# A decoder layer's last MLP pass: the third chunk of columns taken in two halves, its last half finished by VectorE alone

## The chip, the cores and the metric

The kernel runs on one core of a Trainium2 chip. The metric is the device time of one launch in microseconds (us), from runs outside the profiler; one more execution was recorded by the hardware profiler, and its trace is what the rows below come from. TensorE multiplies matrices and writes to PSUM, VectorE and ScalarE work element by element on SBUF and PSUM, GpSimd works on SBUF alone, and SyncE issues most of the DMAs.

## The reference

One layer of a decoder trunk for 1024 prompt tokens and 8 sample tokens: an attention and a convolution branch, a merge, and a squared-ReLU MLP with a norm on either side. The change lies in the last lines, the second MLP product, its norm and the residual sum:

```python
def _rms_norm(x, g):
    xf = x.astype(jnp.float32)
    y = xf * lax.rsqrt(jnp.mean(xf * xf, axis=-1, keepdims=True) + EPS)
    return (y * g.astype(jnp.float32)).astype(x.dtype)
...
    x = x + _rms_norm(mix, g_mix_post)
    h = _rms_norm(x, g_ffn_pre)
    f = jnp.square(jax.nn.relu(h @ w_ff1)) @ w_ff2
    return x + _rms_norm(f, g_ffn_post)
```

`w_ff1` is 1024 x 4096 and `w_ff2` 4096 x 1024. All data are float32.

## The kernel before, in words

Everything is kept transposed: a tile has 128 features as partitions and tokens as columns. The 1032 tokens (`T`) are three chunks of 344 columns (`CH`), and the 1024 output features are eight blocks of 128 (`m` from 0 to 7). So that products come out in float32 precision, each weight and each activation is split into a high and a low part, and each product of 128 features is three matmuls (`mac`, lines 257, 260 and 261): high by high, high by low, low by high.

The second MLP product sums over 4096 hidden features. It is taken in 15 passes of `ff2`. The first 14 take 256 hidden features each and go block by block, chunk by chunk, each adding into the SBUF tile `f`. The last pass (`chunk_major`) takes the last 512 hidden features and goes chunk by chunk: for a chunk it runs the eight blocks in order, so that a chunk of `f` is complete when its eighth block is. For one block of one chunk (`one`), TensorE runs 12 matmuls of 344 columns into one of four PSUM banks, and VectorE adds the bank to `f` (line 1419). ScalarE then squares the block (line 1387) and scales it by the gain (line 1433). The squares of the blocks are added into two running sums (line 1393; of blocks 2 and 4 on GpSimd in the first two chunks, elsewhere on VectorE; in the third chunk blocks 6 and 7 are not added, but summed by TensorE as they are).

When a chunk is complete, `finish` normalises it and writes it out. TensorE sums the squares over the features, with the 344 columns as three blocks of 128 (`sum_rows`, line 304); a chain of tiny VectorE operations and a square root on ScalarE make the factor per token (`rms_rows`, lines 315 to 325); TensorE spreads the factors over all partitions (`spread`, line 331). Then, in four steps of two feature blocks each, VectorE multiplies by the factor (line 1458), the residual is added (line 1461; on GpSimd or VectorE, by step) and SyncE issues the DMA to the output (line 1462). `finish` is a generator: for the first two chunks it is stepped once after each block of the next chunk, so its work stands between the blocks of the next chunk in every engine's queue. For the third chunk nothing comes after it, and it runs by itself at the end.

`pin` and `pe` keep the written order on each engine. `tick` moves the stream of weights along: it issues loads, and splits loaded weights into high and low parts (lines 177 and 180) ahead of their use. `r2` and `r4` hold factors per token that were made in earlier passes by `mlp_factors`.

Of the kernel before, what the change touches and what calls it, by code (L numbers as in the profile page):

```python
# [10 lines left out]
F32 = mybir.dt.float32  # L11
F32R = mybir.dt.float32r
AF = mybir.ActivationFunctionType
OP = mybir.AluOpType
# [4 lines left out]
P = 128  # L19
KT = 8  # L20
NQ = 1024
NB = 8
T = NQ + NB
CH = T // 3
HT = T // 2
ST = HT // 2
EPS = 1e-6
NEG = -1e30

def chunk(c):  # L30
    return slice(c * CH, (c + 1) * CH)
# [6 lines left out]
def tile_decoder_layer(  # L38
# [5 lines left out]
    nc = tc.nc  # L44
# [7 lines left out]
    small = ctx.enter_context(tc.tile_pool(name="small", bufs=2))  # L52
    mm = ctx.enter_context(tc.tile_pool(name="mm", bufs=1, space=PSUM))
# [50 lines left out]
    for i in range(0, KT, 2):  # L104
        m = 36 + 3 * i
# [21 lines left out]
    sums = {}  # L127
# [28 lines left out]
    for key in plan:  # L156
        keys, fs = forms_of(key)
# [141 lines left out]

    NB3 = ((0, 128), (128, 128), (CH - 128, 128))  # L300

    def sum_rows(ps, sq, first, last):
        for b, (o, w) in enumerate(NB3):
            pe(nc.tensor.matmul(ps[:, b:b + 1], sq[:, o:o + w], ones, start=(first and b == 0),  # L304
                                stop=(last and b == 2), skip_group_check=True))

    def rms_rows(ps, s2=None, s4=None):


        var = small.tile([P, 3], F32, name="var")  # L310
        ri = small.tile([P, 3], F32, name="ri")
        if s2 is None:
            pin(nc.vector.tensor_scalar(var, ps[:, 0:3], 1.0 / NQ, EPS, op0=OP.mult, op1=OP.add))
        else:
            pin(nc.vector.tensor_tensor(var, ps[:, 0:3], s4, op=OP.mult))
            pin(nc.vector.tensor_scalar(var, var, EPS, None, op0=OP.add))
        sd = small.tile([P, 3], F32, name="sd")
        pin(nc.scalar.activation(sd, var, AF.Sqrt))
        pin(nc.vector.reciprocal(ri, sd))
        t = small.tile([P, 3], F32, name="nt")  # L320
# [7 lines left out]
    def spread(ri):  # L328
        rb = bank(at, [P, 512], "ps_rb")
        for b, (o, w) in enumerate(NB3):  # L330
# [1041 lines left out]

    with tc.tile_pool(name="ff", bufs=1, side="right") as ff:
        f = ff.tile([P, KT, T], F32, name="f")
        r2 = [ff.tile([P, 3], F32, name=f"r2_{c}") for c in range(3)]
        r4 = [ff.tile([P, 3], F32, name=f"r4_{c}") for c in range(3)]

        def squares_of(src, last=KT):


            res = [None, None]
            for k in range(KT):
                new = k < 2 or k >= last
                nm = "fac" if new else "fsq"
                pool, bufs = (ff, 2) if len(spaces) < 3 else (spaces[2][0], 8)
                sq = pool.tile([P, CH], F32, name=nm, tag=nm, bufs=bufs)
# [9 lines left out]
        def add_sums(ps, tiles, first=True, last=True):  # L1396
            for i, a in enumerate(tiles):
                sum_rows(ps, a, first and i == 0, last and i == len(tiles) - 1)

        def ff2(prs, chunk_major):  # L1400
            hs = [hidden.pop(pr) for pr in prs]
            ws = {}

            def one(m, c):
                ps = bank(mm, [P, CH], "ps_mm")
                if m % 4 == 0 and c == 0:
                    ws[m // 4] = [take(("wf2", 2 * pr + a, m // 4)) for pr in prs for a in range(2)]
                mac(ps, [((w[0][:, m % 4], w[1][:, m % 4]), (rh[:, a, chunk(c)], rl[:, a, chunk(c)]))
                         for w, (a, (rh, rl)) in zip(ws[m // 4], ((a, h) for h in hs for a in range(2)))])
                if m % 4 == 3 and c == 2:  # L1410
                    for w in ws[m // 4]:
                        retire(w)
                if chunk_major or (3 * m + c) % 2:
                    tick()
                d = f[:, m, chunk(c)]
                if prs[0] == 0:
                    nc.scalar.copy(d, ps)
                else:
                    pin(nc.vector.tensor_tensor(d, ps, d, op=OP.add))  # L1419
            if not chunk_major:  # L1420
                for m in range(KT):
                    for c in range(3):
                        one(m, c)
                return
            done = iter(())
            for c in range(3):
                end = c == 2
                sq = squares_of(lambda k: f[:, k, chunk(c)], 6 if end else KT)
                for m in range(KT):
                    one(m, c)  # L1430
                    sums = next(sq)
                    fm = f[:, m, chunk(c)]
                    pin(nc.scalar.activation(fm, fm, AF.Copy, scale=gn[:, 3, m:m + 1]))  # L1433
                    run(done, 1)
                    if end and m == 6:
                        ps = bank(at, [P, 512], "ps_ss")
                        add_sums(ps, sums[:2], True, False)
                run(done)
                if not end:
                    ps = bank(at, [P, 512], "ps_ss")  # L1440
                done = finish(c, ps, sums)
            run(done)

        def finish(c, ps, sums):
            end = c == 2
            if end:
                add_sums(ps, sums[2:], False)
            else:
                yield
                add_sums(ps, sums)  # L1450
            ri = rms_rows(ps, r2[c], r4[c])
            if not end:
                yield
            rb = spread(ri)[:, None, 0:CH].to_broadcast([P, 2, CH])
            vs_ = [f[:, k:k + 2, chunk(c)] for k in range(0, KT, 2)]

            def scale(j):
                pin(nc.vector.tensor_tensor(vs_[j], vs_[j], rb, op=OP.mult))  # L1458

            def out(j, eng):  # L1460
                pin(eng.tensor_tensor(vs_[j], vs_[j], x2[c][:, 2 * j:2 * j + 2, :], op=OP.add))  # L1461
                pin(nc.sync.dma_start(yT[:, 2 * j:2 * j + 2, chunk(c)], vs_[j]))
            scale(0)
            out(0, nc.gpsimd)
            yield
            scale(1)
            out(1, nc.gpsimd)
            yield
            scale(2)
            out(2, nc.vector if end else nc.gpsimd)  # L1470
            yield
            scale(3)
            out(3, nc.vector)
            yield

        def mlp_factors(c):

            for sums in squares_of(lambda k: x2[c][:, k, :]):
                yield
            pin(nc.gpsimd.tensor_tensor(sums[0], sums[0], sums[1], op=OP.add))  # L1480
            yield
            yield
            ps = bank(at, [P, 512], "ps_ss")
            add_sums(ps, sums[0:1])
            ri = rms_rows(ps)
            pin(nc.vector.tensor_tensor(r2[c], ri, ri, op=OP.mult))
            pin(nc.vector.scalar_tensor_tensor(r4[c], r2[c], 1.0 / NQ, r2[c], op0=OP.mult, op1=OP.mult))
# [94 lines left out]
```

## Time and profile before

| | before |
|---|---|
| median of 3 runs | 2033.48 us (2033.07 to 2035.68) |
| the profiled execution, its own time | 2032.52 us |
| its span, first to last instruction | 2030.7 us, so 1.8 us of its time lie around it |
| busy in the span: TensorE, VectorE, ScalarE, GpSimd | 1955.0, 1243.6, 735.3, 602.6 us |
| mean granted TensorE clock | 0.983 of full |

Busy time is the time in which an engine worked on an instruction; matmuls are pipelined, so that a matmul's duration is longer than the distance to the next one's start. The second number of a row of the timeline is a duration in us; "x2" are two instructions in one row, with the time from the first's start to the last's end.

### The profile page before, as it was taken

Reading aid. Unit: us, or ns where it says so; the run is one execution under the profiler, and the core shown is the slowest. Engines: PE = TensorE matmul, PEld = TensorE weight load, DVE = VectorE, ACT = ScalarE, POOL = GpSimd, SP = SyncE. Lnnn points to the kernel's source line nnn. Section 1 sums busy time; section 2 is a strip of 40 time slices with the busy share of each in tenths; the row PEclk is TensorE's granted clock in tenths of the full one; section 3 lists DMA queues with packets and bytes.
Section 4 is the critical chain, followed back from the end, with each engine's and each line's share of the span. In section 5 each row is a group of like instructions: output and inputs, shape, how many; then the busy total and the mean of one; then the engine's idle time right before and its main releaser. Section 6 shows DMA issues by size and latency. Waiting matters only on the chain. (4 is left out here: it accounts for less than half of the span.)

```text
span 2030.7 us, 33252 instructions
## 1 busy us (share of the span) xinstructions
PE 1955.0 (96%) x13253; PEld 1932.2 (95%) x13253; DVE 1243.6 (61%) x2086; ACT 735.3 (36%) x1448; POOL 602.6 (30%) x487
## 2 busy tenths in 40 slices
PE   7999999999998899999999999999999999999996
PEld 6999999999998799999999999999999999999995
DVE  7688768777756787897554423735544444454545
ACT  4355435544442333333343333452222222222242
POOL 3233313332334674662412222211111111111113
PEclk8999999999999899999999999999999999999998
DMA  4221343144334363331665431322222322222102
GB/s 146 59 87 38 108 131 128 59 129 131 111 101 164 113 205 109 126 116 54 186 251 165 138 102 46 94 91 86 84 94 84 125 94 84 94 94 83 53 22 84
DMA packets 85995, 216.74 MB, mean 107 GB/s; under 512 B 12000, under 2 KB 22368, under 8 KB 84944
## 3 DMA queue, kind: packets, MB, share of 16 engines
q1 hardware_dynamic: 68736, 119.12, 18.2%
q10 hardware_dynamic: 8112, 68.78, 10.0%
q0 software_dynamic: 8992, 26.72, 4.4%
q8 instruction: 104, 1.70, 0.3%
q14 instruction: 51, 0.42, 0.1%
HBM read 184.17 MB, written 84.86 MB: 132 GB/s over the span
## 5 line engine op out<-in xcount | busy, mean ns | idle before, releaser
L180 POOL TENSOR_TENSOR wl<-wr,wh 128x512 fp32r<-128x512 f32 x152 | 201.9, 1329 | 804.4 <-ACT wh L177 707.6
L177 ACT CAST wh<-wr 128x512 fp32r<-128x512 f32 x320 | 195.3, 619 | 526.5 <-PE ps_mm L260 272.4
L257 PE MATMUL ps_mm<-hh,wh 128*128 128x344 f32 x1008 | 329.7, 327 | 2.5 <-ACT hh L346 1.9
L260 PE MATMUL ps_mm<-hl,wh 128*128 128x344 f32 x1008 | 324.2, 322 | 3.7 <-DVE hl L340 1.9
L261 PE MATMUL ps_mm<-hh,wl 128*128 128x344 f32 x1008 | 323.4, 321 | 0.0
L261 PE MATMUL ps_mm<-rh,wl 128*128 128x344 f32 x768 | 246.4, 321 | 0.0
L257 PE MATMUL ps_mm<-rh,wh 128*128 128x344 f32 x768 | 246.4, 321 | 0.0
L260 PE MATMUL ps_mm<-rl,wh 128*128 128x344 f32 x768 | 245.7, 320 | 0.0
L260 PE MATMUL ps_mm<-gl,wh 128*128 128x344 f32 x768 | 244.9, 319 | 0.8 <-DVE gl L1303 0.8
L257 PE MATMUL ps_mm<-gh,wh 128*128 128x344 f32 x768 | 245.5, 320 | 0.0
L261 PE MATMUL ps_mm<-gh,wl 128*128 128x344 f32 x768 | 244.7, 319 | 0.0
L1419 DVE TENSOR_TENSOR f<-ps_mm,f 128x344 f32<-128x344 f32 x336 | 170.4, 515 | 111.5 <-PE ps_mm L261 110.9
L180 DVE TENSOR_TENSOR wl<-wr,wh 128x512 fp32r<-128x512 f32 x168 | 139.7, 832 | 152.8 <-ACT wh L177 152.4
L260 PEld LDWEIGHTS ps_mm<-hl,wh 128*128 128x128 f32 x1008 | 190.8, 189 | 5.7 <-DVE hl L340 3.2
L257 PEld LDWEIGHTS ps_mm<-hh,wh 128*128 128x128 f32 x1008 | 191.2, 190 | 3.9 <-ACT hh L346 2.9
L261 PEld LDWEIGHTS ps_mm<-hh,wl 128*128 128x128 f32 x1008 | 190.7, 189 | 0.0
L260 PEld LDWEIGHTS ps_mm<-gl,wh 128*128 128x128 f32 x768 | 144.2, 188 | 1.2 <-DVE gl L1303 1.1
L260 PEld LDWEIGHTS ps_mm<-rl,wh 128*128 128x128 f32 x768 | 144.8, 189 | 0.0
L261 PEld LDWEIGHTS ps_mm<-rh,wl 128*128 128x128 f32 x768 | 144.8, 189 | 0.0
L257 PEld LDWEIGHTS ps_mm<-rh,wh 128*128 128x128 f32 x768 | 144.8, 189 | 0.0
L257 PEld LDWEIGHTS ps_mm<-gh,wh 128*128 128x128 f32 x768 | 144.3, 188 | 0.0
L261 PEld LDWEIGHTS ps_mm<-gh,wl 128*128 128x128 f32 x768 | 144.1, 188 | 0.0
(326 smaller groups left out, 4555.0 us busy)
## 6 DMA issues: line engine op xcount, KB each, us to landing
wr<-in_win_dram SPq DMA_DIRECT2D x152, 256.0 KB
wr<-in_wf_dram SPq DMA_DIRECT2D x128, 256.0 KB
out_okv_dram<-in_cache_dram ACTq DMA_DIRECT2D x16, 1020.0 KB
kt<-in_cache_dram SPq DMA_DIRECT2D x32, 256.0 KB
x_sb<-in_xT_dram SPq DMA_DIRECT2D x12, 344.0 KB
cv_d<-D SPq DMA_DIRECT2D x16, 258.0 KB
gr<-g_d POOLq DMA_DIRECT2D x8, 516.0 KB, 7.4
cv<-cv_d ACTq DMA_DIRECT2D x8, 516.0 KB
```

What stands on the lines that cost most here:

```text
L177: pin_(nc.scalar.copy(hi, raw))
L180: pin_(eng.tensor_tensor(lo, raw, hi.bitcast(F32), op=OP.subtract))
L257: ins = nc.tensor.matmul(ps, wh, rh, start=(first and i == 0), stop=False)
L260: nc.tensor.matmul(ps, wh, rl, start=False, stop=False)
L261: nc.tensor.matmul(ps, wl, rh, start=False, stop=(last and i == n - 1))
L1419: pin(nc.vector.tensor_tensor(d, ps, d, op=OP.add))
```

## The change

The third chunk becomes two pieces of 172 columns (`HC`), so the last pass has four pieces (`LAST`): two of 344 columns and two of 172. Each half runs its own eight blocks, its own sums (two blocks of columns, the second 44 wide) and its own `finish`; that of the first half is stepped between the blocks of the second half. In both halves all four residual additions are VectorE's; the first two chunks keep theirs. Only the last half keeps the third chunk's treatment of the squares, while the first half adds the squares of blocks 2 and 4 on GpSimd as the first two chunks do. The call of `tick` moves from before VectorE's addition into `f` to after it, in all 15 passes.

```diff
-    def sum_rows(ps, sq, first, last):
-        for b, (o, w) in enumerate(NB3):
+    def sum_rows(ps, sq, first, last, blocks=NB3):
+        for b, (o, w) in enumerate(blocks):
...
+        HC = CH // 2
+        HB = ((0, 128), (HC - 128, 128))
+        LAST = [(0, 0, CH, NB3, slice(0, 3)), (1, 0, CH, NB3, slice(0, 3)),
+                (2, 0, HC, HB, slice(0, 2)), (2, HC, HC, HB, slice(2, 4))]
...
-                if chunk_major or (3 * m + c) % 2:
-                    tick()
-                d = f[:, m, chunk(c)]
+                d = f[:, m, s]
...
-            for c in range(3):
-                end = c == 2
-                sq = squares_of(lambda k: f[:, k, chunk(c)], 6 if end else KT)
+            for j, (c, o, n, blocks, fs) in enumerate(LAST):
+                end = j == len(LAST) - 1
+                s = slice(CH * c + o, CH * c + o + n)
+                sq = squares_of(lambda k: f[:, k, s], 6 if end else KT, n)
                 for m in range(KT):
-                    one(m, c)
+                    one(m, s, j == 0, end)
+                    tick()
                     sums = next(sq)
...
-            scale(0)
-            out(0, nc.gpsimd)
-            yield
...
-            out(2, nc.vector if end else nc.gpsimd)
-            yield
-            scale(3)
-            out(3, nc.vector)
-            yield
+            for j in range(4):
+                scale(j)
+                out(j, nc.vector if n < CH or j == 3 else nc.gpsimd)
+                yield
```

On VectorE, the end of the program before: eight rows from the addition of the last two blocks on (`ps_mm` is a block's bank, `ps_ss` the sums, `ps_rb` the spread factors, `x_2` the residual of the third chunk).

```order
L321 SCALAR_TENSOR_TENSOR nt<-ri 128x3
L323 TENSOR_TENSOR ri<-ri,r_2_14351 128x3
L324 TENSOR_TENSOR nt<-nt,var 128x3
L325 SCALAR_TENSOR_TENSOR ri<-nt,ri 128x3
L1458 TENSOR_TENSOR f<-f,ps_rb 128x2x344 x3
L1461 TENSOR_TENSOR f<-f,x_2_12969 128x2x344
L1458 TENSOR_TENSOR f<-f,ps_rb 128x2x344
L1461 TENSOR_TENSOR f<-f,x_2_12969 128x2x344
```

On VectorE now, two blocks in the middle of the second half, where the first half's `finish` is stepped.

```order
L1424 TENSOR_TENSOR f<-ps_mm,f 128x172
L1399 TENSOR_TENSOR fac<-fac,fsq 128x172
L1467 TENSOR_TENSOR f<-f,ps_rb 128x2x172
L1470 TENSOR_TENSOR f<-f,x_2_12969 128x2x172
L1424 TENSOR_TENSOR f<-ps_mm,f 128x172
L1399 TENSOR_TENSOR fac<-fac,fsq 128x172
L1467 TENSOR_TENSOR f<-f,ps_rb 128x2x172
L1470 TENSOR_TENSOR f<-f,x_2_12969 128x2x172
```

A round of block, square sum, scaling and residual now stands four times on VectorE in the second half, and the program ends with four pairs of scaling and residual of two times 172 columns in place of the eight rows' last six operations.

On GpSimd, the end of the program before.

```order
L1461 TENSOR_TENSOR f<-f,x_0_12967 128x2x344 x2
L1393 TENSOR_TENSOR fac<-fac,fsq 128x344
L1461 TENSOR_TENSOR f<-f,x_0_12967 128x2x344
L1461 TENSOR_TENSOR f<-f,x_1_12968 128x2x344 x3
L1461 TENSOR_TENSOR f<-f,x_2_12969 128x2x344 x2
```

And now.

```order
L1470 TENSOR_TENSOR f<-f,x_0_12967 128x2x344 x2
L1399 TENSOR_TENSOR fac<-fac,fsq 128x344
L1470 TENSOR_TENSOR f<-f,x_0_12967 128x2x344
L1399 TENSOR_TENSOR fac<-fac,fsq 128x172
L1470 TENSOR_TENSOR f<-f,x_1_12968 128x2x344 x2
L1399 TENSOR_TENSOR fac<-fac,fsq 128x172
L1470 TENSOR_TENSOR f<-f,x_1_12968 128x2x344
```

GpSimd's last operation was a residual addition of the third chunk; now it is one of the second chunk, which stands beside the blocks of the first half.

## Rows read from the trace of the kernel before

**Rows 1.** The page's costliest groups: one kind of MLP matmul and its idle time.
```profile
L257 PE MATMUL ps_mm<-rh,wh 128*128 128x344 f32 x768 | 246.4, 321 | 0.0
```

**Rows 2.** The chain of work that ended last, parts of it: start, us, what.
```profile
1996.58 0.16 PE ps_mm L260
...
2009.13 0.29 PE ps_mm L260
...
2012.54 0.02 issue
...
2019.29 1.41 DVE f L1461
```

**Rows 3.** The sequencers' instructions behind the program (L1565): duration in ns min/median/max.
```profile
L1565 POOLq EVENT_SEMAPHORE  x4: 17/17/17, 2030.0 to 2030.6; - x4
L1565 POOLq DRAIN  x3: 40/102/13087, 2016.8 to 2030.4; - x3
L1565 SPq DRAIN  x3: 7/7/7, 2024.8 to 2030.2; - x3
```

**Rows 4.** The same ahead of the program (L1556), GpSimd's alone.
```profile
L1556 POOLq DRAIN  x1: 193/193/193, 0.3 to 0.3; - x1
```

**Rows 5.** Timeline of GpSimd in the last 35 us.
```profile
2004.19 1.63 POOL L1461 TENSOR_TENSOR f<-f,x 128x688 f32<-128x688 f32 x1 [1.30 <-DVE f L1458]
2016.10 3.86 POOL L1461 TENSOR_TENSOR f<-f,x 128x688 f32<-128x688 f32 x2 [10.27 <-DVE f L1458]
```

**Rows 6.** Timeline of SyncE's queue from 2012 us: four DMA issues.
```profile
2017.76 3.66 SPq L1462 DMA_DIRECT2D out_yT_dram<-f  x4
```

**Rows 7.** The DMA view from 2012 to 2031 us, in 40 slices.
```profile
GB/s 0 0 0 0 0 0 0 0 0 0 0 0 0 0 365 368 9 0 98 362 383 327 330 388 333 3 0 0 0 0 0 0 0 0 0 0 0 0 0 0
```

**Rows 8.** Timeline of VectorE from 1978 us: starts, durations, idle time before.
```profile
1979.04 0.52 DVE L1419 TENSOR_TENSOR f<-ps_mm,f 128x344 f32<-128x344 f32 x1 [0.52 <-PE ps_mm L261]
...
1989.09 0.50 DVE L1419 TENSOR_TENSOR f<-ps_mm,f 128x344 f32<-128x344 f32 x1
...
1992.21 0.93 DVE L1419 TENSOR_TENSOR f<-ps_mm,f 128x344 f32<-128x344 f32 x2
1993.85 0.16 DVE L315 TENSOR_TENSOR var<-ps_ss,r 128x3 f32<-128x3 f32 x1 [0.70 <-PE ps_ss L304]
...
1995.85 0.52 DVE L1419 TENSOR_TENSOR f<-ps_mm,f 128x344 f32<-128x344 f32 x1
...
2005.03 1.17 DVE L1393 TENSOR_TENSOR fac<-fac,fsq 128x344 f32<-128x344 f32 x1 [0.56 <-ACT fsq L1387]
...
2010.60 0.52 DVE L1419 TENSOR_TENSOR f<-ps_mm,f 128x344 f32<-128x344 f32 x1 [2.29 <-PE ps_mm L261]
2012.56 0.16 DVE L315 TENSOR_TENSOR var<-ps_ss,r 128x3 f32<-128x3 f32 x1 [1.44 <-PE ps_ss L304]
...
2015.08 2.43 DVE L1458 TENSOR_TENSOR f<-f,ps_rb 128x688 f32<-128x688 f32 x3 [1.05 <-PE ps_rb L331]
```

**Rows 9.** Groups of VectorE's instructions from 1976 to 2021 us, by form.
```profile
L1458 DVE TENSOR_TENSOR f<-f,ps_rb 128x688 f32<-128x688 f32 x12 | 10.2, 859 | 1.1 <-PE ps_rb L331 1.1
L1419 DVE TENSOR_TENSOR f<-ps_mm,f 128x344 f32<-128x344 f32 x15 | 7.6, 510 | 5.3 <-PE ps_mm L261 5.1
...
L315 DVE TENSOR_TENSOR var<-ps_ss,r 128x3 f32<-128x3 f32 x3 | 0.5, 161 | 2.9 <-PE ps_ss L304 2.9
```

**Rows 10.** The same of ScalarE.
```profile
L1387 ACT ACTIVATE fsq<-f 128x344 f32<-128x344 f32 x10 | 4.9, 493 | 14.3 <-DVE f L1419 14.2
...
L318 ACT ACTIVATE sd<-var 128x3 f32<-128x3 f32 x3 | 0.6, 199 | 0.7 <-DVE var L316 0.7
```

**Rows 11.** Timeline of TensorE at 90 us: attention matmuls of 128 columns.
```profile
90.44 0.28 PE L576 MATMUL ps_s<-QS,KS 128*128 128x128 f32 x1
90.55 0.27 PE L577 MATMUL ps_s<-QS,KL 128*128 128x128 f32 x1
```

**Rows 12.** Busy time by stretch; the last three numbers: PEclk, DMA share, GB/s.
```profile
2006.00:2009.00 3.00, 2.75 (x14) 2.75 (x15) 2.28 (x4) 0.62 (x2) 0.00 (x0) 0.69 0.36 134
```

More of the change, by code (lines that the diff above doesn't have):

```diff
@@ L300, in tile_decoder_layer, with rms_rows @@
     NB3 = ((0, 128), (128, 128), (CH - 128, 128))
-    def sum_rows(ps, sq, first, last):
-        for b, (o, w) in enumerate(NB3):
+    def sum_rows(ps, sq, first, last, blocks=NB3):
+        for b, (o, w) in enumerate(blocks):
             pe(nc.tensor.matmul(ps[:, b:b + 1], sq[:, o:o + w], ones, start=(first and b == 0),
[L305 to L311, printed above, removed]
+                                stop=(last and b == len(blocks) - 1), skip_group_check=True))
+    def rms_rows(ps, s2=None, s4=None, n=3):
+        var = small.tile([P, 4], F32, name="var")[:, 0:n]
+        ri = small.tile([P, 4], F32, name="ri")[:, 0:n]
         if s2 is None:
-            pin(nc.vector.tensor_scalar(var, ps[:, 0:3], 1.0 / NQ, EPS, op0=OP.mult, op1=OP.add))
+            pin(nc.vector.tensor_scalar(var, ps[:, 0:n], 1.0 / NQ, EPS, op0=OP.mult, op1=OP.add))
         else:
-            pin(nc.vector.tensor_tensor(var, ps[:, 0:3], s4, op=OP.mult))
+            pin(nc.vector.tensor_tensor(var, ps[:, 0:n], s4, op=OP.mult))
             pin(nc.vector.tensor_scalar(var, var, EPS, None, op0=OP.add))
-        sd = small.tile([P, 3], F32, name="sd")
+        sd = small.tile([P, 4], F32, name="sd")[:, 0:n]
         pin(nc.scalar.activation(sd, var, AF.Sqrt))
         pin(nc.vector.reciprocal(ri, sd))
-        t = small.tile([P, 3], F32, name="nt")
+        t = small.tile([P, 4], F32, name="nt")[:, 0:n]
         pin(nc.vector.scalar_tensor_tensor(t, ri, -0.5, ri, op0=OP.mult, op1=OP.mult))
@@ L326, in rms_rows, with spread @@
         return ri
-    def spread(ri):
+    def spread(ri, blocks=NB3):
         rb = bank(at, [P, 512], "ps_rb")
-        for b, (o, w) in enumerate(NB3):
+        for b, (o, w) in enumerate(blocks):
             pe(nc.tensor.transpose(rb[:, o:o + w], ri[:, b:b + 1].to_broadcast([P, P]), ident))
@@ L1374, in tile_decoder_layer, with squares_of @@
         f = ff.tile([P, KT, T], F32, name="f")
-        r2 = [ff.tile([P, 3], F32, name=f"r2_{c}") for c in range(3)]
-        r4 = [ff.tile([P, 3], F32, name=f"r4_{c}") for c in range(3)]
-        def squares_of(src, last=KT):
+        HC = CH // 2
+        HB = ((0, 128), (HC - 128, 128))
+        LAST = [(0, 0, CH, NB3, slice(0, 3)), (1, 0, CH, NB3, slice(0, 3)),
+                (2, 0, HC, HB, slice(0, 2)), (2, HC, HC, HB, slice(2, 4))]
+        r2 = [ff.tile([P, 4], F32, name=f"r2_{c}") for c in range(3)]
+        r4 = [ff.tile([P, 4], F32, name=f"r4_{c}") for c in range(3)]
+        def squares_of(src, last=KT, n=CH):
             res = [None, None]
@@ L1394, in squares_of, with add_sums @@
                 yield res
-        def add_sums(ps, tiles, first=True, last=True):
+        def add_sums(ps, tiles, first=True, last=True, blocks=NB3):
             for i, a in enumerate(tiles):
-                sum_rows(ps, a, first and i == 0, last and i == len(tiles) - 1)
+                sum_rows(ps, a, first and i == 0, last and i == len(tiles) - 1, blocks)
         def ff2(prs, chunk_major):
@@ L1402, in ff2, with one @@
             ws = {}
-            def one(m, c):
-                ps = bank(mm, [P, CH], "ps_mm")
-                if m % 4 == 0 and c == 0:
+            def one(m, s, first, last):
+                w_ = s.stop - s.start
+                ps = bank(mm, [P, CH], "ps_mm")[:, 0:w_]
+                if m % 4 == 0 and first:
                     ws[m // 4] = [take(("wf2", 2 * pr + a, m // 4)) for pr in prs for a in range(2)]
-                mac(ps, [((w[0][:, m % 4], w[1][:, m % 4]), (rh[:, a, chunk(c)], rl[:, a, chunk(c)]))
+                mac(ps, [((w[0][:, m % 4], w[1][:, m % 4]), (rh[:, a, s], rl[:, a, s]))
                          for w, (a, (rh, rl)) in zip(ws[m // 4], ((a, h) for h in hs for a in range(2)))])
-                if m % 4 == 3 and c == 2:
+                if m % 4 == 3 and last:
                     for w in ws[m // 4]:
                         retire(w)
-                if chunk_major or (3 * m + c) % 2:
-                    tick()
-                d = f[:, m, chunk(c)]
+                d = f[:, m, s]
                 if prs[0] == 0:
@@ L1422, in ff2 @@
                     for c in range(3):
-                        one(m, c)
+                        one(m, chunk(c), c == 0, c == 2)
+                        if (3 * m + c) % 2:
+                            tick()
                 return
             done = iter(())
-            for c in range(3):
-                end = c == 2
-                sq = squares_of(lambda k: f[:, k, chunk(c)], 6 if end else KT)
+            for j, (c, o, n, blocks, fs) in enumerate(LAST):
+                end = j == len(LAST) - 1
+                s = slice(CH * c + o, CH * c + o + n)
+                sq = squares_of(lambda k: f[:, k, s], 6 if end else KT, n)
                 for m in range(KT):
-                    one(m, c)
+                    one(m, s, j == 0, end)
+                    tick()
                     sums = next(sq)
-                    fm = f[:, m, chunk(c)]
+                    fm = f[:, m, s]
                     pin(nc.scalar.activation(fm, fm, AF.Copy, scale=gn[:, 3, m:m + 1]))
@@ L1436, in ff2 @@
                         ps = bank(at, [P, 512], "ps_ss")
-                        add_sums(ps, sums[:2], True, False)
+                        add_sums(ps, sums[:2], True, False, blocks)
                 run(done)
@@ L1440, in ff2, with finish @@
                     ps = bank(at, [P, 512], "ps_ss")
-                done = finish(c, ps, sums)
+                done = finish(LAST[j], s, ps, sums, end)
             run(done)
-        def finish(c, ps, sums):
-            end = c == 2
+        def finish(piece, s, ps, sums, end):
+            c, o, n, blocks, fs = piece
             if end:
-                add_sums(ps, sums[2:], False)
+                add_sums(ps, sums[2:], False, True, blocks)
             else:
                 yield
-                add_sums(ps, sums)
-            ri = rms_rows(ps, r2[c], r4[c])
+                add_sums(ps, sums, True, True, blocks)
+            ri = rms_rows(ps, r2[c][:, fs], r4[c][:, fs], len(blocks))
             if not end:
                 yield
-            rb = spread(ri)[:, None, 0:CH].to_broadcast([P, 2, CH])
-            vs_ = [f[:, k:k + 2, chunk(c)] for k in range(0, KT, 2)]
+            rb = spread(ri, blocks)[:, None, 0:n].to_broadcast([P, 2, n])
+            vs_ = [f[:, k:k + 2, s] for k in range(0, KT, 2)]
             def scale(j):
@@ L1483, in mlp_factors @@
             ps = bank(at, [P, 512], "ps_ss")
[L1484 to L1487, printed above, removed]
+            blocks = NB3 if c < 2 else HB + tuple((HC + o, w) for o, w in HB)
+            n = len(blocks)
+            add_sums(ps, sums[0:1], blocks=blocks)
+            ri = rms_rows(ps, n=n)
+            q2, q4 = r2[c][:, 0:n], r4[c][:, 0:n]
+            pin(nc.vector.tensor_tensor(q2, ri, ri, op=OP.mult))
+            pin(nc.vector.scalar_tensor_tensor(q4, q2, 1.0 / NQ, q2, op0=OP.mult, op1=OP.mult))
         for pr in range(NP - 2):
```

10 lines of the change are left out of this document (3 added, 7 removed).

## Prediction

> **What bounds the kernel now.** I read the page first. TensorE is busy in 96% of the span, and in the MLP its matmuls wait for nothing: the 768 of one kind have 0.0 us of idle time before them [rows 1]. So the move of `tick`, which only swaps a weight's split with an addition on VectorE, lies behind a TensorE that never waits, and I cost it at nothing; if that cover were gone, a late split would cost one VectorE operation, 0.5 us, per pass.
>
> All else happens in the last 40 us, and there the chain of waits comes next. In the third chunk it runs through VectorE, not TensorE, and it ends with VectorE's last residual addition, 2019.29 + 1.41 = 2020.70 [rows 2]. The span goes on for 10.0 us behind that. Two things lie there. SyncE waits for the output: its last issue ends at 2021.42 [rows 6], the last packets move at about 2023.9 (slice 24 of 40 from 2012) [rows 7], and its drain comes at 2024.8. But the others wait for GpSimd, whose closing drain, issued at 2016.8, takes 13.09 us, to 2029.9; its release follows at 2030.0 and SyncE's next step at 2030.2 [rows 3]. So the output's landing has some 5 us to spare, and GpSimd's drain ends the span. At the start of the program, where GpSimd had done four small fills, its drain took 0.19 us [rows 4]. The long one was issued while its last two additions ran, which end at 2016.10 + 3.86 = 2019.96 [rows 5]: 9.97 us from there to its end.
>
> **The change part by part.** *TensorE.* The third chunk's 96 matmuls of 344 columns, 0.16 us apart [rows 2], become 192 of 172. None of that width is in the trace. Below, half of 0.16 is 0.08; above, 0.16 as now. The nearest rows are matmuls of 128 columns that stand 0.11 apart, each with a weight load of its own [rows 11], more than 128/344 of 0.16 (0.06); so there is a floor, and I take 0.11. TensorE's work grows from 15.4 to 21.1 us. It is hidden as long as VectorE's round for a block takes longer than 12 x 0.11 = 1.32 us.
>
> *VectorE, one operation.* 0.161 us at 3 columns, 0.510 at 344, 0.859 at 688 [rows 9]: a fixed 0.16 and 1.01 ns per column. So 172 columns cost 0.34, two times 172 cost 0.51, and halving is far from half price. Two additions start 0.42 apart (0.93 for two of 0.51) [rows 8], so the next begins 0.09 before the end where it needs no result. ScalarE's square is 0.493 at 344 and 0.199 at 3 [rows 10]: 0.35 at 172. A step to another engine takes 0.03 (0.02 [rows 2], read to 10 ns).
>
> *The walk along VectorE*, from the third chunk's first addition at 1992.21, ahead of which nothing changes, by the measured distances [rows 8]:
> (a) That addition to the sums' `var`: 1.64 before. The sums stand behind the second block's matmuls, which end 0.55 earlier: 1.1.
> (b) `var` to the third block: 2.00; ScalarE's work ahead of the root shrinks: 1.8.
> (c) Third to seventh block with the chunk before being finished beside them: the same list of operations ran in the second chunk in 1989.09 - 1979.04 = 10.05. Shorter are four additions and one square sum by 0.17 each and one square by 0.15: 9.0. GpSimd's two square sums halve too, and a VectorE addition of two SBUF operands ends only after GpSimd's (1.17 us at 2005.03, to 2006.20; GpSimd's ends at 2005.82 [rows 5, 8]): between 8.6 and 9.0, I take 8.9.
> (d) Seventh block to the next piece's first: 3.12, twice 0.49 less: 2.1. The second half begins at 2006.1.
> (e) Its opening as (a) and (b): 2.9, to 2009.0.
> (f) Four rounds of addition 0.34, square 0.35, square sum 0.34, scaling and residual 0.51 each, with three steps of 0.03 and two overlaps of 0.09 (the scaling and the next addition need no result of the one before): 2.0 each, to 2017.0. GpSimd does nothing here, so no addition is held up.
> (g) Seventh to eighth block: the sums and TensorE's twelve matmuls come first, 1.0. (h) Eighth to `var`: 1.96 before, with shorter operations 1.35. (i) `var` to the first scaling: 2.52 before with the slower spread, 2.2. (j) Four pairs of scaling and residual, 0.98 each and an overlap: 4.0. That makes 2025.6 at TensorE's full clock.
>
> TensorE's clock was not full at this place: in 2006 to 2009 the granted clock is 0.69, and the eighth block's matmuls are 0.29 apart, the 1.2 GHz level instead of 2.4, after TensorE had waited for the last square sum [rows 2, 12]. The halves bring the same wait there, and less work beside it (1.32 of 2.0 us). I take the low level there again: 12 x 0.11 = 1.3 more for the eighth block and, as an estimate, 0.4 for sums and spread: VectorE ends at 2027.3, 6.6 us later than before. The bounds are 2025.3 (full clock, GpSimd's bound in (c) low) and 2030.5 (matmuls at 0.16, worked out below).
>
> *The tail.* GpSimd's last operation is now a residual addition of the second chunk, at about 2003. If its drain runs on for 10 us, or 13 from its issue, it is done by 2016. Then the output's landing ends the span. Each half transfer has 176 KB and comes a microsecond behind the one before, so none queues. From VectorE's end: issue and first packet 0.9 (issue 2017.76, packets in slice 14, from 2018.65 [rows 6, 7]), moving 0.5 to 1.0 (344 KB took two slices of 0.475), to SyncE's drain 0.9 (2023.9 to 2024.8), closing steps 0.8 (2029.9 to 2030.7): 3.1 to 3.6, I take 3.5, where it was 10.0. The tail gives back 6.5.
>
> One page bears on this term. The Trainium skill ("VectorE: DVE Perf Modes", section "The DRAIN you can't avoid") says that the drains around a program are boilerplate of a constant 12 ns or so on every engine; GpSimd's here is 13,087 ns [rows 3]. By that page nothing would be given back with GpSimd's work, and the sum would be that of the second case below.
>
> **Sum:** + 6.6 - 6.5 = + 0.1, a span of 2030.8. The profiled execution's own time, 2032.52, lies 1.0 below the median of the runs, so I forecast against the median: 2033.48 + 0.1 = 2033.6. What a measurement of this kernel can tell from no change is about 0.2%, 4.1 us.
>
> **The rivals.**
> 1. *The forecast: VectorE loses what GpSimd's drain gives back.* For it: the operations' fixed 0.16 us, and two waits of GpSimd's drain that fit its own last work. Own range 2031.5 to 2036.5: low with full clock (- 1.8), high with more stretches at 1.2 GHz or rounds of 2.2 us. 68%.
> 2. *Slower: the drain follows the output's landing*, not GpSimd's own work. Before, it ended 6.0 after the last packets (2029.9 - 2023.9) and 5.1 after SyncE's drain. It decides if that gap stays: the end is then 5.1 later than forecast, 2038.7. Against it: the drain's row names nothing to wait for, and it was issued 5 us before the landing. 14%.
> 3. *Slower: TensorE becomes the bound.* From 0.167 us per matmul on, twelve take longer than VectorE's round of 2.0. At 0.16 openings and eighth block lose 0.55 each and the first half's eight blocks (15.4) outlast VectorE's 13.9 of (a) to (d): 3.2 more, 2036.8. At 1.2 GHz throughout, twice 0.11, the 16 blocks take 42.2 us where (a) to (g) have 25.8; less the 1.3 counted already and the 2.6 of a block that TensorE is ahead, that is 12.3 more, 2045.9. For it: the low clock at the end; against it: the 0.11 at 128 columns. 11%.
> 4. *Faster: halves at half price.* If 172 columns cost half of 344 on both engines, a round loses 0.44, (j) 0.7, and (a) to (e) and (h) some 1.5; with full clock VectorE ends at 2021.5, and the time is 2027.8. Against it: the 0.16 us of three columns. 7%.
>
> **How the numbers follow.** The time is the first case's. The range 2031.0 to 2039.0 takes in the first two cases and the lower part of the third; the fourth and the third's upper part, with little of the rest, stay out. Faster by over 4.1 us: the fourth case and a tail of the first, 0.09. Slower: the second for the most part, half of the third, a tail of the first: 0.23. Within: 0.68.
>
> **What would show it.** GpSimd's closing drain must end before SyncE's, and the span some 0.8 us after SyncE's last wait. The 172-column matmuls should start 0.11 apart, VectorE's additions take 0.34, the second half's rounds 2.0, and VectorE should end about 2027. A drain that ends 5 us after SyncE's shows case two; a VectorE that waits for TensorE in the rounds, case three. The forecast is wrong in its main step if the time is right but VectorE's end and the drain are not where I put them.

## The result, and the profile after

The changed kernel takes 2048.12 us (median of 14 runs, 2034.33 to 2051.28) where the kernel before, in the same comparison, takes 2035.84 (14 runs, 2032.75 to 2038.88). The ratio is 1.0055, 95% interval 1.0042 to 1.0068: it is slower, by some 11 us by the ratio and 12.3 by the medians. The forecast was 2033.6 and its range ended at 2039.0.

The profiled execution after took 2050.01 us. Its page, two lines (the span; the granted clock in 40 slices of 51 us, in tenths of full speed):

```profile
span 2048.2 us, 33506 instructions
...
PEclk8999999999998999999999999999999999999995
```

The last digit is the finding: 5 tenths for the whole last slice, half of full speed. The view of busy time by stretch shows where that begins (columns: stretch, length, busy time and count of PE, PEld, DVE, ACT, POOL, then the granted clock, DMA share, GB/s):

```profile
1995.00:1998.00 3.00, 2.69 (x25) 2.61 (x24) 1.55 (x6) 2.44 (x7) 0.00 (x0) 1.00 0.08 27
1998.00:2005.00 7.00, 6.63 (x34) 6.41 (x33) 3.31 (x10) 1.75 (x6) 2.70 (x3) 0.52 0.16 53
...
2010.00:2017.00 7.00, 7.00 (x34) 7.00 (x34) 2.03 (x6) 2.36 (x6) 0.00 (x0) 0.50 0.16 56
...
2022.00:2032.00 10.00, 10.00 (x49) 10.00 (x49) 6.19 (x16) 3.14 (x8) 0.00 (x0) 0.50 0.18 54
```

Full to 1998, 0.52 in the next 7 us (0.3 us at full rate and the rest at half), then 0.50 to the end: the 1.2 GHz level in place of 2.4. Before, the clock had fallen only near the third chunk's end [rows 12]. In the last two stretches TensorE is busy in every microsecond, and yet the clock stays at half. TensorE's timeline at the three places (start, duration, and in brackets the idle time ahead and what ended it):

```profile
1993.16 0.28 PE L261 MATMUL ps_mm<-rh,wl 128*128 128x172 f32 x1
1993.27 0.28 PE L257 MATMUL ps_mm<-rh,wh 128*128 128x172 f32 x1
...
1996.34 0.83 PE L304 MATMUL ps_ss<-ones,fac 128*128 128x1 f32 x6 [0.30 <-DVE fac L1399]
...
1999.11 0.90 PE L331 MATMUL ps_rb<-ident,ri 128*128 128x128 f32 x3 [0.36 <-DVE ri L325]
...
2005.07 0.42 PE L260 MATMUL ps_mm<-rl,wh 128*128 128x172 f32 x1
2005.29 0.42 PE L261 MATMUL ps_mm<-rh,wl 128*128 128x172 f32 x1
```

Ahead of the fall the new matmuls of 172 columns start 0.11 us apart, as forecast; behind it 0.21 to 0.22. Between lie the second chunk's sums (twelve matmuls of one column) with a wait of 0.30 us for the last square sum among them, and then the fall at 1998.3; a second wait, 0.36 us for the factors that are spread, follows it. What that does to VectorE (its timeline: first addition of the first half, first of the second half, two rounds, the eighth block, the last operation):

```profile
1996.20 0.57 DVE L1424 TENSOR_TENSOR f<-ps_mm,f 128x172 f32<-128x172 f32 x2
...
2015.34 0.34 DVE L1424 TENSOR_TENSOR f<-ps_mm,f 128x172 f32<-128x172 f32 x1 [1.47 <-PE ps_mm L261]
...
2025.09 0.34 DVE L1424 TENSOR_TENSOR f<-ps_mm,f 128x172 f32<-128x172 f32 x1 [0.86 <-PE ps_mm L261]
...
2027.65 0.34 DVE L1424 TENSOR_TENSOR f<-ps_mm,f 128x172 f32<-128x172 f32 x1 [0.50 <-PE ps_mm L261]
...
2037.04 0.34 DVE L1424 TENSOR_TENSOR f<-ps_mm,f 128x172 f32<-128x172 f32 x1 [3.93 <-PE ps_mm L261]
...
2044.62 0.52 DVE L1470 TENSOR_TENSOR f<-f,x 128x344 f32<-128x344 f32 x1
```

A round lasts 2027.65 - 2025.09 = 2.56 us, which is 12 x 0.213, and VectorE waits for TensorE in each. Before, VectorE's work set that pace [rows 2, 8]. Now the chain of work that ended last runs through the matmuls (start, us, what):

```profile
2026.97 0.21 PE ps_mm L257
2027.18 0.21 PE ps_mm L260
```

VectorE's own operations are not longer than forecast (groups of its instructions from 1996 to 2047 us, by form: busy time, mean ns | idle before):

```profile
L1424 DVE TENSOR_TENSOR f<-ps_mm,f 128x172 f32<-128x172 f32 x16 | 5.3, 335 | 16.1 <-PE ps_mm L261 16.1
...
L1467 DVE TENSOR_TENSOR f<-f,ps_rb 128x344 f32<-128x344 f32 x8 | 4.0, 505 | 0.8 <-PE ps_rb L331 0.8
```

16.1 us of waiting for TensorE stand ahead of 16 additions that take 5.3. In the tail, the sequencers' instructions behind the program (L1569, durations in ns, first and last start; they answer to [rows 3]) and GpSimd's last operation (its timeline):

```profile
L1569 SPq EVENT_SEMAPHORE  x12: 17/28/28, 2045.6 to 2048.2; - x12
...
L1569 POOLq DRAIN  x3: 40/93/11982, 2006.3 to 2048.0; - x3
L1569 SPq DRAIN  x3: 7/7/7, 2047.4 to 2047.7; - x3
```

```profile
2006.61 1.66 POOL L1470 TENSOR_TENSOR f<-f,x 128x688 f32<-128x688 f32 x1
```

GpSimd's closing drain runs from 2006.3 for 11.98 us, to 2018.3, which is 10.0 behind its last operation's end at 2008.27. Before, it was 9.9 by the same reading (2016.8 + 13.09 - 19.96, where the prediction has 9.97) [rows 3, 5]. It is out of the way, and the span ends 3.1 us behind VectorE (2045.14 to 2048.2) in place of 10.0.

The two executions can be laid beside each other from the first addition of the third chunk: 1992.21 before, 1996.20 after. The 4.0 us ahead of it are not put down to the change: in the ten traces of this document that addition starts at 1992.21 to 1997.09 where the kernel before or a variant of it ran, and at 1991.05 to 1996.24 where the halves ran. From there to VectorE's end it was 28.5 us before and is 48.9 now: 20.4 lost, 6.9 given back in the tail, and 13.5 us net, as 2050.01 - 2032.52 - 4.0 says too.

### The profile page after: what moved, and what is told of

It is laid out like the page before. It is cut to its first block, busy times and chain, and to the rows that moved or that the text cites. A ratio compares the mean times of both kernels' runs of the same rounds, so it can differ in the third digit from the quotient of the medians.

```text
span 2048.2 us, 33506 instructions
## 1 busy us (share of the span) xinstructions
PE 1979.9 (97%) x13352; PEld 1957.5 (96%) x13352; DVE 1244.0 (61%) x2115; ACT 739.4 (36%) x1465; POOL 599.6 (29%) x487
## 3 DMA queue, kind: packets, MB, share of 16 engines
q8 instruction: 105, 1.72, 0.4%
## 5 line engine op out<-in xcount | busy, mean ns | idle before, releaser
L261 PE MATMUL ps_mm<-rh,wl 128*128 128x344 f32 (+1 forms) x800 | 260.7, 326 | 0.0
L257 PE MATMUL ps_mm<-rh,wh 128*128 128x344 f32 (+1 forms) x800 | 260.7, 326 | 0.0
L260 PE MATMUL ps_mm<-rl,wh 128*128 128x344 f32 (+1 forms) x800 | 259.9, 325 | 0.0
L1424 DVE TENSOR_TENSOR f<-ps_mm,f 128x344 f32<-128x344 f32 (+1 forms) x344 | 172.1, 507 | 129.7 <-PE ps_mm L261 129.4
L257 PEld LDWEIGHTS ps_mm<-rh,wh 128*128 128x128 f32 x800 | 157.9, 197 | 0.0
L260 PEld LDWEIGHTS ps_mm<-rl,wh 128*128 128x128 f32 x800 | 157.9, 197 | 0.0
L261 PEld LDWEIGHTS ps_mm<-rh,wl 128*128 128x128 f32 x800 | 157.9, 197 | 0.0
```

The costliest lines, as they stand in the source:

```text
L257: ins = nc.tensor.matmul(ps, wh, rh, start=(first and i == 0), stop=False)
L260: nc.tensor.matmul(ps, wh, rl, start=False, stop=False)
L261: nc.tensor.matmul(ps, wl, rh, start=False, stop=(last and i == n - 1))
```

## The experiments

The theory is that the clock makes the loss. A short wait of TensorE beside the narrow matmuls costs it the full rate, at 1.2 GHz the narrow ones no longer fit under VectorE's round, and at full rate the halves would come out even. Its form 1a is that a wait is needed to lose the clock; the other form is that narrowness alone loses it. The rivals: the halves' operations cost VectorE more than was forecast; twice as many matmuls cost as such; and, for the tail, GpSimd's drain follows the output's landing and not its own work.

**Only the moved `tick`** (kernel before, nothing else changed):

```diff
-                if chunk_major or (3 * m + c) % 2:
-                    tick()
...
                         one(m, c)
+                        if (3 * m + c) % 2:
+                            tick()
...
                     one(m, c)
+                    tick()
                     sums = next(sq)
```

> The kernel before with the moved call alone: the stream of weights is moved along behind VectorE's addition instead of ahead of it, in all 15 passes. Theory: TensorE never waits in the MLP, so no change, within 2 us. Rival (splits come late and TensorE waits for weights): idle time ahead of the MLP's matmuls in the trace, and up to 0.5 us in each of 14 passes, 7 us slower.

Measured: 2034.98 us, ratio 0.9993 (0.9982 to 1.0004), no difference. The MLP's matmuls still wait for nothing (a group of TensorE's instructions; after the second bar the idle time ahead of them):

```profile
L257 PE MATMUL ps_mm<-rh,wh 128*128 128x344 f32 x768 | 246.3, 321 | 0.0
```

**Only the narrow matmuls** (kernel before; each block of the third chunk is computed as two times 172 columns into one bank, all else is whole):

```diff
-                mac(ps, [((w[0][:, m % 4], w[1][:, m % 4]), (rh[:, a, chunk(c)], rl[:, a, chunk(c)]))
-                         for w, (a, (rh, rl)) in zip(ws[m // 4], ((a, h) for h in hs for a in range(2)))])
+                for o in (range(0, CH, CH // 2) if chunk_major and c == 2 else (None,)):
+                    s = chunk(c) if o is None else slice(CH * c + o, CH * c + o + CH // 2)
+                    mac(ps if o is None else ps[:, o:o + CH // 2], [((w[0][:, m % 4], w[1][:, m % 4]), (rh[:, a, s], rl[:, a, s]))
+                        for w, (a, (rh, rl)) in zip(ws[m // 4], ((a, h) for h in hs for a in range(2)))])
```

> The kernel before, with one thing of the change alone: each block of the third chunk is 24 matmuls of 172 columns instead of 12 of 344, into the same bank; VectorE, ScalarE, GpSimd and the finish are those of before. TensorE's blocks then take 24 x 0.11 = 2.6 us at full clock, so TensorE runs through the third chunk almost without waiting. Theory 1a (narrow work loses the clock only behind a wait, and does not get it back): no wait comes before the seventh block's sums, the clock stays full until then, and the time is that of before plus the low clock of the eighth block, 24 x 0.21 = 5.1 instead of 3.4: 0 to 4 us above before. Theory 1b (narrow work alone lets the clock fall): up to 8 blocks at 5.1 us, some 15 to 20 us above before. Theory 2 (the number of matmuls costs the 12 us whatever the clock): some 12 us above before at full clock.

Measured: 2037.83 us, ratio 1.0004 (0.9994 to 1.0013). TensorE's timeline, and its busy time by stretch:

```profile
2005.06 0.27 PE L257 MATMUL ps_mm<-rh,wh 128*128 128x172 f32 x1
2005.17 0.28 PE L260 MATMUL ps_mm<-rl,wh 128*128 128x172 f32 x1
```

```profile
2000.00:2010.00 10.00, 10.00 (x93) 10.00 (x91) 5.97 (x14) 3.23 (x6) 3.33 (x2) 1.00 0.11 38
```

0.11 apart at a full clock for ten microseconds. The only wait of TensorE among these blocks stands at their end (0.53 us, at 2018.08). So neither the doubled count nor narrowness alone loses anything, and form 1b is out. That a wait is needed, form 1a, agrees with this run; whether a wait is enough, the next run but one shows.

**The whole chunk, finished by VectorE alone** (kernel before; GpSimd does none of the third chunk's residual additions):

```diff
             scale(0)
-            out(0, nc.gpsimd)
+            out(0, nc.vector if end else nc.gpsimd)
             yield
             scale(1)
-            out(1, nc.gpsimd)
+            out(1, nc.vector if end else nc.gpsimd)
```

> The kernel before with one part of the change alone: the third chunk stays whole, and all four of its residual additions are VectorE's. Theory (GpSimd's closing drain runs 10 us on from GpSimd's own last operation): that operation is now the second chunk's, which ended at 2005.8, so the drain is over at 2016 and the output's landing ends the span. VectorE's finish gets longer, 4 x (0.86 + 0.03 + 0.88 - 0.09) = 6.7 from 2015.1, to 2021.8, and 3.1 to 3.5 follow: a span of some 2025, 5 to 6 us under the kernel before. Rival (the drain follows the landing, whoever adds): the landing comes 1 us later, and the time is 1 us above before.

Measured: 2027.97 us against 2035.12, ratio 0.9968 (0.9955 to 0.9980): faster. GpSimd's last operation, VectorE's last, and the sequencers' drains behind the program:

```profile
2004.56 1.63 POOL L1461 TENSOR_TENSOR f<-f,x 128x688 f32<-128x688 f32 x1 [1.30 <-DVE f L1458]
```

```profile
2020.75 0.87 DVE L1461 TENSOR_TENSOR f<-f,x 128x688 f32<-128x688 f32 x1
```

```profile
L1565 POOLq DRAIN  x3: 40/93/11636, 2004.5 to 2025.1; - x3
L1565 SPq DRAIN  x3: 7/7/7, 2024.5 to 2024.8; - x3
```

The drain ends at 2004.5 + 11.64 = 2016.1, 10 us behind GpSimd's last operation (2006.19) and ahead of VectorE's end at 2021.62, so ahead of the last output. Nothing of it follows the landing. The span, 2025.3, ends 3.7 behind VectorE. This half of the change alone wins some 7 us (6.5 by the ratio), and the halving loses more than that. The same run also shows a clock that comes back (busy time by stretch):

```profile
2009.00:2011.00 2.00, 2.00 (x10) 2.00 (x9) 0.35 (x1) 0.79 (x2) 0.00 (x0) 0.50 0.49 176
2011.00:2014.00 3.00, 1.40 (x10) 1.23 (x9) 1.15 (x8) 1.27 (x3) 0.00 (x0) 0.95 0.00 0
```

TensorE had waited 1.72 us for a square sum, up to 2006.62, and the clock had fallen to half. Its next matmuls were 344 wide, and by 2011 to 2014 it had nearly all of the clock again.

**Halves, with GpSimd in the last one** (changed kernel; the last half's first two residual additions go back to GpSimd):

```diff
-                out(j, nc.vector if n < CH or j == 3 else nc.gpsimd)
+                out(j, nc.vector if j == 3 or (n < CH and not (end and j < 2)) else nc.gpsimd)
```

> The changed kernel with the first two residual additions of the last half given back to GpSimd. Theory: GpSimd's last addition then ends about when VectorE's does, and its drain runs 10 us on from there, 7 us behind the end of the changed kernel: 2055 in runs with TensorE's low clock. Rival (GpSimd's drain costs nothing by itself): within 1 us of the changed kernel.

Measured: 2049.81 us (2037.73 to 2056.68), ratio 1.0073 (1.0051 to 1.0094). GpSimd's last operations and the drains:

```profile
2032.51 2.05 POOL L1470 TENSOR_TENSOR f<-f,x 128x344 f32<-128x344 f32 x2 [25.16 <-DVE f L1467]
```

```profile
L1569 POOLq DRAIN  x3: 40/93/11632, 2032.9 to 2045.0; - x3
L1569 SPq DRAIN  x3: 7/7/7, 2038.1 to 2044.8; - x3
```

The drain ends at 2044.5, once more 10.0 behind GpSimd's last operation (2034.56), and SyncE, done at 2038.1, waits for it. The trace decides the tail. The time is a blurred answer: the median is only 1.7 us above the changed kernel's, since the runs spread by 19 us with their mean clock (0.979 in the profiled one, which fell late; 0.974 in that of the change). The four runs at 0.973 to 0.975 took 2052.5 to 2056.68 us, where the change's at 0.974 took 2048.7 to 2051.28: some 4 us more, in the direction of the 7 that were expected.

The late fall is a finding of its own. Up to the last half this program is the changed kernel's, and TensorE waits at the same two places, 0.31 us at the second chunk's sums and 0.53 at the spread. Yet the clock stays full through the whole first half, and falls only at about 2013.7, behind three more waits (0.32, 0.33 and 0.83 us). TensorE's wait at the sums, busy time by stretch, and VectorE's first additions of the two halves:

```profile
1996.37 0.83 PE L304 MATMUL ps_ss<-ones,fac 128*128 128x1 f32 x6 [0.31 <-DVE fac L1399]
```

```profile
1998.00:2005.00 7.00, 6.47 (x59) 6.32 (x59) 4.99 (x14) 2.96 (x10) 3.83 (x4) 1.00 0.15 53
...
2014.00:2026.00 12.00, 12.00 (x58) 12.00 (x58) 6.07 (x15) 3.20 (x9) 0.00 (x0) 0.50 0.20 60
```

```profile
1996.24 0.57 DVE L1424 TENSOR_TENSOR f<-ps_mm,f 128x172 f32<-128x172 f32 x2
...
2010.12 0.57 DVE L1424 TENSOR_TENSOR f<-ps_mm,f 128x172 f32<-128x172 f32 x2
```

So the wait is not enough to lose the clock. And the first half, with its waits, at full clock and with nothing added, takes 2010.12 - 1996.24 = 13.88 us, where the changed kernel's took 19.1 with the clock at half from 1998.3.

**Halves, with TensorE's waits filled** (changed kernel; 34 matmuls of 344 columns, whose result nobody reads, are added where TensorE waited):

```diff
+            def fill(n):
+                ps = bank(at, [P, 512], "ps_fill")[:, 0:CH]
+                for _ in range(n):
+                    pe(nc.tensor.matmul(ps, ws[1][0][0][:, 0], hs[0][0][:, 0, chunk(0)], start=True, stop=True))
...
+                    if j > 1 and m in (1, 2):
+                        fill(6)
                     run(done, 1)
                     if end and m == 6:
+                        fill(10)
+                    if end and m == 6:
```

> The changed kernel with 34 more matmuls of 344 columns that nobody reads, put where TensorE waits in the two halves: 6 ahead of the sums and 6 ahead of the spread of the piece before, in each half, and 10 ahead of the last half's own sums. Theory 1 (clock): the clock stays at 2.4 GHz, the narrow matmuls stand 0.11 apart, and the time is that of the forecast, about that of before, 10 to 14 us under the changed kernel. Theory 2 (count): up to 34 x 0.16 = 5 us slower than the changed kernel.

Measured: 2034.07 us (11 runs, 2032.14 to 2036.26), ratio 0.9994 (0.9985 to 1.0003). More work on TensorE, and 14.05 us less than the changed kernel by the medians, 12.4 by the ratios, each of which was taken against its own runs of the kernel before. Busy time by stretch, and VectorE's timeline in the second half:

```profile
1998.00:2005.00 7.00, 7.00 (x65) 7.00 (x65) 5.70 (x10) 2.36 (x6) 5.29 (x4) 1.00 0.27 101
...
2010.00:2017.00 7.00, 7.00 (x61) 6.91 (x61) 5.35 (x18) 2.47 (x8) 0.00 (x0) 1.00 0.18 53
```

```profile
2012.86 0.34 DVE L1424 TENSOR_TENSOR f<-ps_mm,f 128x172 f32<-128x172 f32 x1
...
2014.84 0.33 DVE L1424 TENSOR_TENSOR f<-ps_mm,f 128x172 f32<-128x172 f32 x1
```

The clock is 1.00 in the same stretches where the changed kernel had 0.52 and 0.50, and a round takes 1.98 us where 2.0 was forecast, with no wait for TensorE. This is the halves as the prediction had them, and they come out even.

**Halves of everything but the matmuls** (changed kernel; each half computes the whole chunk's 344 columns and VectorE reads its own 172, so TensorE does twice the third chunk's work):

```diff
-                ps = bank(mm, [P, CH], "ps_mm")[:, 0:w_]
+                ps = bank(mm, [P, CH], "ps_mm")
+                ms = slice(s.start // CH * CH, s.start // CH * CH + CH)
...
-                mac(ps, [((w[0][:, m % 4], w[1][:, m % 4]), (rh[:, a, s], rl[:, a, s]))
+                mac(ps, [((w[0][:, m % 4], w[1][:, m % 4]), (rh[:, a, ms], rl[:, a, ms]))
...
+                ps = ps[:, s.start - ms.start:s.stop - ms.start]
```

> The changed kernel, with its 192 matmuls of the halves 344 columns wide: each half computes the whole chunk's block and VectorE takes its own half of the bank, so TensorE does all of the third chunk twice. Theory 1 (the time went because narrow matmuls leave TensorE's clock at 1.2 GHz once a pause has taken it there): wide matmuls get the clock back, stand 0.16 apart, and a block takes 1.9 us instead of 2.56, so twice the work is 8 to 11 us faster than the changed kernel, some 1 to 4 us above before. Theory 2 (the doubled number of matmuls and weight loads costs it, whatever the clock): no faster than the changed kernel, or slower.

Measured: 2037.59 us, ratio 1.0016 (1.0007 to 1.0025). TensorE's timeline, and busy time by stretch:

```profile
2005.12 0.32 PE L261 MATMUL ps_mm<-rh,wl 128*128 128x344 f32 x1
2005.28 0.32 PE L257 MATMUL ps_mm<-rh,wh 128*128 128x344 f32 x1
```

```profile
2000.00:2010.00 10.00, 10.00 (x66) 10.00 (x65) 7.23 (x14) 4.07 (x11) 4.37 (x4) 1.00 0.39 143
```

Twice the matmul work is 10.5 us faster than the changed kernel by the medians, 7.9 by the ratios: TensorE, busier, never waits there, and keeps 2.4 GHz in this stretch. Since the clock didn't fall here, the run doesn't show that wide matmuls bring it back, and it doesn't tell apart whether their width or the missing waits kept it.

**A burst in the middle** (changed kernel; one burst of 24 unread matmuls of 344 columns behind the last half's fourth block, with `fill` as above):

```diff
+                    if end and m == 3:
+                        fill(24)
                     run(done, 1)
```

> The changed kernel with one burst of 24 matmuls of 344 columns that nobody reads, behind the fourth block of the last half, and nothing else added. Theory 1 (at 1.2 GHz, narrow matmuls without a pause do not bring the clock back, wide ones do): where the clock is low ahead of the burst, it is back at 2.4 GHz within it, after 3 to 7 us, and the narrow matmuls behind it go from 0.21 to 0.11 apart until TensorE waits again; the burst costs 4 to 7 us and gives back up to 5, so the time is about that of the changed kernel, within 4 us. Rival (the clock does not depend on the matmuls' width, but comes back after some time or not at all): the narrow matmuls behind the burst stay 0.21 apart.

Measured: 2046.15 us, ratio 1.0048 (1.0030 to 1.0065). Busy time by stretch, and the chain around the burst (`ps_fill`):

```profile
2015.00:2020.00 5.00, 5.00 (x25) 5.00 (x25) 2.34 (x10) 0.78 (x2) 0.00 (x0) 0.50 0.00 0
2020.00:2025.00 5.00, 5.00 (x23) 5.00 (x23) 1.54 (x4) 0.78 (x2) 0.00 (x0) 0.65 0.22 70
2025.00:2030.00 5.00, 4.84 (x44) 4.75 (x43) 2.37 (x7) 1.57 (x4) 0.00 (x0) 1.00 0.05 14
```

```profile
2019.68 0.21 PE ps_mm L261
2019.90 5.47 PE ps_fill L1435 x24
...
2025.45 0.11 PE ps_mm L260
```

TensorE is busy throughout at 0.50 with the narrow matmuls. In the burst the clock comes back (0.65 over 5 us is 1.5 us at full rate, so at about 2023.5), and the narrow matmuls behind it stand 0.11 apart again. The burst itself takes 5.47 us of the chain and comes late, so the time gains little, if anything (1.0048 against 1.0055, with intervals that overlap).

**The best version, tried further** (the whole chunk on VectorE, as above; the sums over the two running sums, which hold the squares of the first six blocks, are put behind the eighth block's matmuls):

```diff
-                    if end and m == 6:
+                    if end and m == 7:
                         ps = bank(at, [P, 512], "ps_ss")
```

> The whole third chunk with all its residual additions on VectorE, as in the first experiment, and one edit more: the sums over the two running sums of squares stand behind the eighth block's matmuls on TensorE and not ahead of them. Theory: TensorE no longer waits for the sixth block's square sum ahead of the eighth block (1.7 us before) and so keeps its clock there; the eighth block's addition follows the seventh's on VectorE, 2 to 2.5 us earlier, and the time is 2 us or more below that of the first experiment, some 9 us below before. Rival (VectorE's round decides the eighth block anyway): no faster than the first experiment.

Measured: 2026.29 us against 2035.99, ratio 0.9949 (0.9935 to 0.9962), the fastest of all. VectorE's timeline at that place:

```profile
2008.48 0.93 DVE L1419 TENSOR_TENSOR f<-ps_mm,f 128x344 f32<-128x344 f32 x2
2012.03 0.16 DVE L315 TENSOR_TENSOR var<-ps_ss,r 128x3 f32<-128x3 f32 x1 [2.62 <-PE ps_ss L304]
```

The seventh and eighth additions now follow each other, and the clock is full there (1.00 from 2006 to 2010), but the wait moves on to the sums (2.62 us; 1.44 before [rows 8]). The spans of the two profiled executions are alike (2025.1 and 2025.3), and the two ratios' intervals overlap, so the 2 us that were expected are not shown, and whether the late sums gain anything over the run without them stays open.

## Why the prediction was wrong

**The failed step is the clock.** The prediction said of the low clock "I take the low level there again": for the eighth block alone, 1.3 us and 0.4 for sums and spread. It carried one stretch of [rows 12] over to the one place that looked alike. It didn't ask what the new waits do at the *start* of the halves, where step (a) itself puts the sums behind a block that ends earlier, nor how TensorE gets out of the low level afterwards. Measured, the clock was at half from 1998.3 to the end, and with it went the overlap: a block's twelve matmuls, 1.32 us that were to hide under a round of 2.0, took 2.56 and set the pace. From the first addition to the second half's first the way was 19.1 us (forecast 13.9), and from there to VectorE's end 29.8 (forecast 21.2): 5.2 and 8.6, together 13.8 us that the sum lacked.

**The third rival had it.** Its upper part, 1.2 GHz throughout with 0.22 per matmul, gave 2045.9, 12.3 above the forecast (its terms, 42.2 - 25.8 - 1.3 - 2.6, make 12.5); the measured extra is 13.8 in the trace. It was left outside the range, with only a part of the rival's 11%, and with "the 0.11 at 128 columns" against it: a row at full clock, which can't say whether the clock stays full. Its lower part, matmuls 0.16 apart at full clock, gave 2036.8, 3.3 above the median; the run with 344-wide matmuls in the halves, which is that case, measured a ratio of 1.0016, 3.3 us. The trace agrees: 37.9 us from the first addition to VectorE's end, where that walk has 38.3 (2030.5 - 1992.21).

**The rest of the walk held.** VectorE's 172 columns took 0.335 us (forecast 0.34), two times 172 0.505 (0.51), the square 0.347 (0.35), and the matmuls stood 0.11 apart. At full clock and with nothing added (the run with GpSimd in the last half) the first half took 13.88 us (forecast 13.9), and part by part 2.77, 8.99 and 2.12 for (a) with (b), (c) and (d), where 2.9, 8.9 and 2.1 were forecast; so this is not luck. With the waits filled, rounds were 1.98 (2.0), and from the first addition to VectorE's end it was 34.9 us where the forecast at full clock was 33.4 (2025.6 - 1992.21). The excess lies in the first half (0.7) and from the seventh to the eighth block (0.8), where added matmuls stand. At full clock the forecast's sum is 1.6 us under the median (2025.6 in place of 2027.3); the ratio 0.9994 is 1.2 under, and its interval reaches from 3.1 under to 0.6 over.

**The tail held.** The forecast gave back 6.5 us, the trace 6.9. GpSimd's drain ends 9.9 to 10.0 us behind its own last operation in all ten traces, and in the run with the whole chunk on VectorE it ends ahead of the last output, which rules the second rival out. The Trainium skill ("VectorE: DVE Perf Modes", section "The DRAIN you can't avoid") calls the drains around a program a constant of some 12 ns; here GpSimd's long one takes 11,632 to 13,087 ns in the four kernels shown. By that rule nothing is given back, and the sum would have been 2033.48 + 6.6 = 2040.1, not the second case's 2038.7 as the prediction has it. Where the drain ends decides 6 to 7 us of the span.

**Nothing for the `tick`** held (0.9993). The fourth rival, halves at half price, fell with the 335 ns.

By the ratios the account is: the third chunk finished by VectorE alone - 6.5 us (0.9968), the halving at full clock + 5.3 (from 0.9968 to 0.9994, with the added matmuls in it), the clock + 12.4 (from 0.9994 to 1.0055): + 11.2.

**What takes the clock down is not settled.** The wait ahead of the fall, 0.30 us, costs next to nothing by itself. In the traces of the last pass every fall stands behind waits of TensorE, and the three whose TensorE doesn't wait at the second chunk's sums (filled, wide, and narrow alone) keep the clock there. But of the three that do wait there two lose it (the change, and the burst, 0.31 us up to 1991.18), and one keeps it (GpSimd in the last half, 0.31 us up to 1996.37), though its rows up to the place of the fall are those of the change, some 0.03 us later. So these runs show no fall without a wait, and that the same wait doesn't always bring one. The executions outside the profiler agree: of the changed kernel's 14 runs two took 2034.33 and 2039.04 us, at mean clocks of 0.984 and 0.981 where the others had 0.974 to 0.977. What makes it come or not is open.

## What to carry to other kernels

Ahead of halving a tile, work out TensorE's time for a block at 1.2 GHz too, with the spacing as it stands then: if it no longer fits under the other engines' round, a fraction of a microsecond's wait can, though it need not, cost the full clock for all that follows. Look in the profile for what the last operation of each engine is and how long its closing drain runs on, since moving GpSimd's last operations to VectorE was worth some 7 us alone, with the operations themselves longer on the path. Change one thing at a time: here one half of the edit won 7 us and the other hid it.

## What the runs showed that was not expected

- Here a TensorE without a gap did not get its clock back by that. It ran narrow matmuls at 1.2 GHz, busy 7.00 of 7.00 and 10.00 of 10.00 us, until the second half was done, while 344-wide ones had it back within a few microseconds (in the whole chunk by 2011 to 2014, in the burst before it ended). Where the clock was full, narrow matmuls kept it, busy 10.00 of 10.00 us. The Trainium skill ("TensorE: Matmul & The Clock Gate", section "The HAM clock gate") files 1.2 GHz under idle and 2.4 GHz under busy; by the busy time that the trace records, these rows differ from that.
- Matmuls of 172 columns stand 0.11 us apart at full clock, the same as those of 128 [rows 11], and 0.213 at half. Those of 344 go from 0.16 only to 0.29 [rows 2]. So half the width costs 0.7 of the time at either level, and what holds the narrow ones back was not tested apart.
- Added work that nobody reads made the kernel faster: 34 wide matmuls by 12.4 us and a doubled chunk by 7.9, by the ratios.
